# Up projection: ten column-tile pairs in seven block products, with their weight sums on GpSimd

## The chip, the core and the metric

The kernel runs on one core of one Trainium2 chip. Such a core has TensorE (PE: matmuls, with its weight loads listed apart as PEld), VectorE (DVE), ScalarE (ACT), GpSimd (POOL) and SyncE (SP, which here only issues DMAs). Each takes its own instructions in a fixed order and waits for the others through semaphores. The metric is the device time of one execution in microseconds, lower is better.

## The reference

One decoder layer on 512 tokens of 1024 channels, in float32. The part that the change touches is the channel mixer at the end:

```python
u2 = _rmsnorm(h, norm2_g[l])
z = _causal_dwconv(u2 @ w_ffn_up[l], ffn_dw_w[l], ffn_dw_b[l])
h = h + (jax.nn.silu(z[..., :FFN_DIM]) * z[..., FFN_DIM:]) @ w_ffn_down[l]
return _rmsnorm(h, final_g)
```

`w_ffn_up` is 1024 x 5632 (twice FFN_DIM = 2816), the convolution has width 3 along the tokens, `w_ffn_down` is 2816 x 1024. Before it come a norm, one input projection, a convolution branch with width 31, four heads of chunked gated linear attention, a gated merge of both branches and an output projection; of these the change touches only the end of the last attention head.

## The kernel before

**Precision.** A matmul is made of three matmuls in the fp32r format (`mm3`, L305): each operand is split into a rounded part `hi` and a rest `lo`, and lo x hi, hi x lo and hi x hi are added up in a PSUM bank. A weight tile of 128 x 1024 is loaded (`load`, L167, one 512 KB DMA into a `raw` tile, 4 buffers), then split by ScalarE (`whi`, L266) and VectorE (`wlo`, L267) in `split_weight`. The list `order` (L147 to L161) holds all weight tiles in the order of use; `weight` (L276) hands out the next one and splits two further ahead.

**Up projection.** It works on channels as rows and tokens as columns. `col_tile` (L313) makes one 128-channel column tile of the result: 8 blocks of the contraction, 3 matmuls each, all 512 tokens as the moving operand, so 24 matmuls of 128x512. Column tile i of the silu half and tile FT + i (FT = 22) of the gate half belong together: `glu` (L1106) runs the width-3 convolution (`ffn_conv`, L1098: one ScalarE instruction reading PSUM, two VectorE instructions), the silu and the product. The 22 pairs are taken in twos, (p, q): `first_of_pair` and `second_of_pair` (L1120, L1128) also build the sums of token halves that the down projection needs. There are three groups of such twos (`GROUPS`, L34: 4, 3 and 4 of them). After each group follows its part of the down projection.

**Down and output projection.** These already use the seven products of Strassen and Winograd in place of eight block products: `seven` (L979) with the steps a11, a12, s1, n2, s4, n3, a22. Their weight sums are made by DMAs that add while they write (issued by GpSimd, L208 and L225) and by VectorE (L218).

**Start of the up projection.** The first two (0, 2) is special (L1211 to L1220). Its four weight tiles are split beforehand, three of its four column tiles are made in token halves (128x256 matmuls) because the last tokens of `u2` arrive late (`to_channels`, L382, at the first halves of tiles 1 and 2), and the fourth is made whole:

```python
for j, lo in [(j, lo) for lo in (0, H) for j in range(3)]:
    ...
    col_tile(ws[j], acts2, accs[j], lo, lo + H, at)
col_tile(ws[3], acts2, accs[3])
```

**Order.** The code is written in one program order; a scheduler decides at compile time how the instructions of each engine follow each other, and the hardware then keeps that order. Where no `manual_schedule` or `issue_after` binds it, an instruction of a later line may be put ahead of an earlier one that is not ready in the scheduler's own reckoning.

**The last head.** `gated` (L875) transposes the head's output in two halves, the first into one of 5 `mm` PSUM banks, the second into one of 3 `ax` banks. At its last call (L916) four `mm` banks hold gate tiles (L906 to L915), so the next column tile (`w_gla`, L926) gets the bank of that first half.

**The end.** `Finish` (L1145) norms rows of the result: square sums on ScalarE, the gain product on VectorE, the root on GpSimd, then the scaling in two parts and a store. The last row block's last half is done in two pieces (L1027 to L1033). `gain3`, the final gain, is loaded at L1096, before the up projection.

Of the kernel before, what the change touches and what calls it, by code (L numbers as in the profile page):

```python
# [66 lines left out]
def trunk_layer(ctx: ExitStack, tc: tile.TileContext, a: dict, out: bass.AP):  # L67
# [55 lines left out]
    pp = cp.tile([P, PP_N], F32, name="pp")  # L123
    gate_up = cp.tile([P, HEADS * DK], F32R, name="gate_up")
    ones = cp.tile([P, P], F32, name="ones")
# [3 lines left out]
    keep = cp.tile([P, P], U8, name="keep")  # L129
    att = cp.tile([P, NT, P], F32, name="att")  # L130

# [27 lines left out]
    for gi, pairs in enumerate(GROUPS):  # L159
        order += [("w_up", j) for pair in pairs for i in pair for j in (i, FT + i)]  # L160
        order += [("w_down", (pairs, step, d)) for step, d in STEPS]  # L161
    ready, raws = [], []
    kept = {}
    used = [0]
    pace = [None]

    def load():  # L167
        if len(raws) < len(order):
            name, j = order[len(raws)]
            if name in SEVEN:  # L170
                raws.append(load_block(name, *j))
                return
            raw = raw_tile()
            nc.sync.dma_start(raw, a[name][j])
            raws.append(raw)

    def raw_tile():
        return wp.tile([P, D], F32, tag="raw", name=nm("raw"), bufs=4)
# [42 lines left out]
    def sum_on(name, pairs, step, d):  # L221

        if step in ("a11", "n2"):
            nxt = block(name, pairs, d, *((0, 1) if step == "a11" else (1, 0)))
            nc.gpsimd.dma_start(kept[pairs, d], nxt, accum_op=ALU.add)  # L225

    def split_weight(halves=False, between=None):

        if len(ready) < len(order):
            while len(raws) <= len(ready):  # L230
                load()
            raw = raws[len(ready)]
            name, spec = order[len(ready)]
            if name in SEVEN:
                raw = operand(raw, *spec)
# [5 lines left out]
                sum_on(name, *spec)  # L241
                ready.append((hi, lo))
                load()
                return
            hi = wp.tile([P, D], F32R, tag="whi", name=nm("whi"), bufs=4)
            if order[len(ready)][0] == "w_low":
                nc.scalar.copy(hi, raw)
                if order[len(ready)][1] == 0:
                    part_lo = lambda t: t.rearrange("p (k c) -> p k c", c=P)[:, :, :RANK]
                    nc.vector.tensor_tensor(part_lo(hi), part_lo(raw), part_lo(hi.bitcast(F32)), ALU.subtract)  # L250
                ready.append((hi, None))
                load()
                return
            lo = wp.tile([P, D], F32R, tag="wlo", name=nm("wlo"), bufs=4)
            if halves:
                ready.append((hi, lo))

                def high(c):
                    nc.scalar.copy(hi[:, c], raw[:, c])

                def low(c):
                    nc.vector.tensor_tensor(lo[:, c], raw[:, c], hi[:, c].bitcast(F32), ALU.subtract)

                cols = [slice(j * T, (j + 1) * T) for j in range(2)]
                return [[lambda c=c, part=part: part(c) for c in cols] for part in (high, low)]
            nc.scalar.copy(hi, raw)  # L266
            pace[0] = nc.vector.tensor_tensor(lo, raw, hi.bitcast(F32), ALU.subtract)  # L267
            ready.append((hi, lo))
            load()

# [41 lines left out]

    def col_tile(w, acts, acc=None, lo=0, hi=T, at={}):  # L313

        if acc is None:
            acc = mm_bank()
        for k in range(KT):
# [456 lines left out]
    class Head:  # L774
# [99 lines left out]

        def gated(self):  # L875
            for s in range(2):
                po = ax_bank() if s else mm_bank()
                for p in range(NT):
# [20 lines left out]
    for h in range(HEADS + 1):  # L899
# [15 lines left out]
        gate_r(2 * h + 1) if new else gate_b(3)  # L915
    heads[-1].gated()  # L916
    gla_scope.close()
# [61 lines left out]
    def seven(name, pairs, acts, complete, at=lambda step, i: None, fine=False):  # L979
# [31 lines left out]
        while steps:  # L1011
# [6 lines left out]
            for i in range(2):  # L1018
# [76 lines left out]
    ffn_scope, fp = scoped("ffn", 1)  # L1095
    gain3 = load_gain("final_g")  # L1096

# [22 lines left out]
    def first_of_pair(i, accs):  # L1120

        w = fp.tile([P, 3 * H], F32, tag="w", name=nm("w"), bufs=2)
        glu(i, accs, w[:, :T])
# [4 lines left out]
    def second_of_pair(i, accs, w, acts):  # L1128

        f = fp.tile([P, T], F32, tag="f", name=nm("f"), bufs=2)  # L1130
        glu(i, accs, f)
        v = fp.tile([P, 3 * H], F32, tag="v", name=nm("v"), bufs=2)
        s1, n2, s4 = (v[:, c * H : (c + 1) * H] for c in range(3))
# [6 lines left out]
        acts["s1"], acts["n2"], acts["s4"] = y(0), y(1), y(2)  # L1140
        return acts

    SPLIT = 5 * P

    class Finish:  # L1145
# [8 lines left out]
        def part(self, n, c):  # L1154
# [3 lines left out]
            y = self.y[:, n * T + c.start : n * T + c.stop] if self.y else tmp() if self.parts else hn  # L1158
            self.last = nc.vector.tensor_tensor(y, hn, gain3[:, n * T + c.start : n * T + c.stop], ALU.mult)
            self.parts.append((n, y))  # L1160
# [28 lines left out]
    def last_complete(t, n, c):  # L1189
# [3 lines left out]
        if ends[t].width == D and t > 1:  # L1193
            ends[t].scale()
            if t == 3:
                with tc.issue_after(ends[t].last.ins):
                    ends[2].store()
                ends[t].store()

    def last_at(step, i):  # L1200

        if (step, i) == ("a22", 0):
            for t in range(2):
                ends[t].scale()
            for t in range(2):
                ends[t].store()

    for gi, pairs in enumerate(GROUPS):
        acts = []
        early = {}  # L1210
        if gi == 0:  # L1211
# [10 lines left out]
        def both(i):  # L1222
            return early.get(i) or [col_tile(weight("w_up", i), acts2), col_tile(weight("w_up", FT + i), acts2)]

        for p, q in pairs:
            w, found = first_of_pair(p, both(p))
            acts.append(second_of_pair(q, both(q), w, found))
        if gi < len(GROUPS) - 1:
            seven("w_down", pairs, acts, lambda t, n, c: None)
        else:  # L1230
            seven("w_down", pairs, acts, last_complete, last_at, True)
    ffn_scope.close()
# [89 lines left out]
```

## Time and profile before

| | us |
|---|---|
| three timed runs: median (lowest, highest) | 837.88 (837.52, 839.6) |
| the profiled execution, its own device time | 837.71 |
| its span, first to last instruction | 835.9 |
| ScalarE, GpSimd busy in the span | 391.8, 42.9 |
| first two of the up projection, PE from its first matmul to the end of its fourth tile | 481.42 to 505.9 |
| first group's part of the down projection on PE | 571.4 to 609.5 |

The span is 1.8 us shorter than the device time of the same execution; what lies around it is not listed by instruction. In the trace a matmul's duration is from its start to its modelled end, and neighbours overlap: what a matmul costs in a stream is the distance between two starts. The same holds for VectorE and ScalarE, where a new instruction starts 0.06 to 0.1 us before the end that is listed for the one ahead of it.

### The profile page before, as it was taken

Reading aid. Unit: us, or ns where it says so; the run is one execution under the profiler, and the core shown is the slowest. Engines: PE = TensorE matmul, PEld = TensorE weight load, DVE = VectorE, ACT = ScalarE, POOL = GpSimd, SP = SyncE. Lnnn points to the kernel's source line nnn. Section 1 sums busy time; section 2 is a strip of 40 time slices with the busy share of each in tenths; the row PEclk is TensorE's granted clock in tenths of the full one; section 3 lists DMA queues with packets and bytes.
Section 4 is the critical chain, followed back from the end, with each engine's and each line's share of the span. In section 5 each row is a group of like instructions: output and inputs, shape, how many; then the busy total and the mean of one; then the engine's idle time right before and its main releaser. Section 6 shows DMA issues by size and latency. Waiting matters only on the chain.

```text
span 835.9 us, 9981 instructions
## 1 busy us (share of the span) xinstructions
PE 826.8 (99%) x3821; PEld 690.5 (83%) x3821; DVE 651.5 (78%) x927; ACT 391.8 (47%) x544; POOL 42.9 (5%) x65
## 2 busy tenths in 40 slices
PE   9999999999999999999999999999999999999996
PEld 7888888888888888888888898888888888888885
DVE  6689879999998788744688868778757687677795
ACT  6632247437523422449434554444434444444454
POOL 1000000000000100000001000001000010000111
PEclk9999999999999999999999999999999999999999
DMA  8233322222222322222347643234742348322462
GB/s 313 101 102 101 101 99 86 98 79 76 101 76 76 126 100 86 92 101 76 106 96 220 205 155 112 91 98 103 216 150 88 67 89 285 102 84 93 101 125 102
DMA packets 28305, 97.79 MB, mean 117 GB/s; under 512 B 3208, under 2 KB 3344, under 8 KB 28256
## 3 DMA queue, kind: packets, MB, share of 16 engines
q1 hardware_dynamic: 24800, 85.35, 29.6%
q0 software_dynamic: 3456, 11.80, 8.2%
q8 instruction: 30, 0.49, 0.2%
q14 instruction: 19, 0.16, 0.1%
HBM read 95.03 MB, written 2.10 MB: 116 GB/s over the span
## 4 chain that ended last, share of the span: by engine, by line
PE 96%; DVE 1%; ACT 0%; DMA 0%; issue 0%; POOL 0%; POOLq 0%; SPq 0%; ACTq 0%
PE mm L309 29%; PE mm L310 29%; PE mm L311 29%; PE mm L521 3%; PE ax L862 1%; PE ax L310 1%; PE ax L311 1%; PE ax L309 1%; PE ax L864 1%; PE ax L844 1%; PE ax L435 0%; PE ax L831 0%; PE ax L830 0%; DMA x<-in_x_dram 0%; DVE hres L1023 0%
## 5 line engine op out<-in xcount | busy, mean ns | idle before, releaser
L309 PE MATMUL mm<-uh,wlo 128*128 128x512 f32 (+1 forms) x760 | 293.0, 385 | 0.0
L311 PE MATMUL mm<-uh,whi 128*128 128x512 f32 (+1 forms) x760 | 290.8, 383 | 0.0
L310 PE MATMUL mm<-ul,whi 128*128 128x512 f32 (+1 forms) x760 | 290.6, 382 | 0.0
L266 ACT CAST whi<-raw 128x1024 fp32r<-128x1024 f32 x114 | 118.7, 1046 | 125.5 <-PE mm L311 93.6
L267 DVE TENSOR_TENSOR wlo<-raw,whi 128x1024 fp32r<-128x1024 f32 x114 | 138.4, 1218 | 36.7 <-ACT whi L266 36.4
L311 PEld LDWEIGHTS mm<-uh,whi 128*128 128x128 f32 x760 | 142.8, 188 | 27.9
L310 PEld LDWEIGHTS mm<-ul,whi 128*128 128x128 f32 x760 | 142.9, 188 | 27.6
L309 PEld LDWEIGHTS mm<-uh,wlo 128*128 128x128 f32 x760 | 142.9, 188 | 27.6
L615 DVE SCALAR_TENSOR_TENSOR c<-h,pp,c 128x511 f32<-128x511 f32 (+14 forms) x240 | 162.4, 728 | 0.7
L1103 DVE SCALAR_TENSOR_TENSOR tmp<-mm,pp,tmp 128x511 f32<-128x511 f32 x88 | 65.9, 748 | 68.8 <-ACT tmp L1101 67.5
L1101 ACT ACTIVATE tmp<-mm,pp 128x512 f32<-128x512 f32 x44 | 34.3, 780 | 61.8 <-PE mm L311 61.8
L239 ACT CAST whi<-kept 128x1024 fp32r<-128x1024 f32 (+1 forms) x32 | 31.7, 995 | 24.0 <-DVE kept L218 10.6
L240 DVE TENSOR_TENSOR wlo<-kept,whi 128x1024 fp32r<-128x1024 f32 (+1 forms) x32 | 36.6, 1152 | 3.0 <-ACT whi L239 2.8
L1023 DVE TENSOR_TENSOR hres<-hres,mm 128x512 f32<-128x512 f32 (+1 forms) x49 | 32.7, 671 | 5.0 <-PE mm L311 3.3
L239 ACT CAST whi<-raw 128x1024 fp32r<-128x1024 f32 (+1 forms) x24 | 23.7, 995 | 18.0 <-PE mm L311 17.8
L240 DVE TENSOR_TENSOR wlo<-raw,whi 128x1024 fp32r<-128x1024 f32 (+1 forms) x24 | 27.3, 1152 | 2.4 <-ACT whi L239 2.3
L310 PE MATMUL mm<-wlo,sh 128*128 128x512 f32 x66 | 25.8, 391 | 0.0
L311 PE MATMUL mm<-whi,sh 128*128 128x512 f32 x66 | 25.7, 389 | 0.0
L309 PE MATMUL mm<-whi,sl 128*128 128x512 f32 x66 | 25.5, 389 | 0.0
L309 PE MATMUL mm<-h,wlo 128*128 128x512 f32 x64 | 25.0, 391 | 0.4 <-DVE tmp L882 0.4
L310 PE MATMUL mm<-h,whi 128*128 128x512 f32 x64 | 24.9, 389 | 0.0
L311 PE MATMUL mm<-h,whi 128*128 128x512 f32 x64 | 24.9, 389 | 0.0
(258 smaller groups left out, 1127.9 us busy)
## 6 DMA issues: line engine op xcount, KB each, us to landing
raw<-in_w_up_dram SPq DMA_DIRECT2D x44, 512.0 KB, 3.3
raw<-in_w_glu_dram SPq DMA_DIRECT2D x16, 512.0 KB, 3.9
raw<-in_w_down_dram SPq DMA_DIRECT2D x15, 512.0 KB, 3.3
kept<-in_w_down_dram POOLq DMA_DIRECT2D x10, 512.0 KB, 5.4
raw<-in_w_v_dram SPq DMA_DIRECT2D x8, 512.0 KB, 3.8
raw<-in_w_qk_dram SPq DMA_DIRECT2D x8, 512.0 KB, 3.3
raw<-in_w_r_dram SPq DMA_DIRECT2D x8, 512.0 KB, 3.3
raw<-in_w_gb_dram SPq DMA_DIRECT2D x8, 512.0 KB, 3.1
```

The lines of the kernel that those rows point to most:

```text
L239: nc.scalar.copy(hi, raw)
L240: nc.vector.tensor_tensor(lo, raw, hi.bitcast(F32), ALU.subtract)
L266: nc.scalar.copy(hi, raw)
L267: pace[0] = nc.vector.tensor_tensor(lo, raw, hi.bitcast(F32), ALU.subtract)
L309: nc.tensor.matmul(acc, ll, rh, start=first, stop=False, **kw)
L310: nc.tensor.matmul(acc, lh, rl, start=False, stop=False, **kw)
L311: nc.tensor.matmul(acc, lh, rh, start=False, stop=last, **kw)
L521: nc.tensor.matmul(acc, act, ready[k // 2][wi][:, j], start=first, stop=last)
L615: nc.vector.scalar_tensor_tensor(y[:, s:], c[:, : T - s], w, y[:, s:], ALU.mult, ALU.add)
L1023: nc.vector.tensor_tensor(hres[t, n][:, c], hres[t, n][:, c], acc[:, c], op)
L1101: nc.scalar.activation(z, acc, AF.Identity, bias=pp[:, PP_FB + m : PP_FB + m + 1], scale=w[2])
L1103: nc.vector.scalar_tensor_tensor(z[:, s:], acc[:, : T - s], w[j], z[:, s:], ALU.mult, ALU.add)
```

## The change

For ten of the eleven twos (p, q), all but the first, the column tiles q and FT + q are no longer made as two column tiles. Their 1024 x 256 weights are taken as 2 x 2 blocks (halves of the contraction; tile q and tile FT + q) and the activations as 2 x 2 blocks (halves of the contraction; token halves), and seven block products of 12 matmuls 128x256 take the place of eight. Tiles p and FT + p stay plain. The products are interleaved in program order with half tiles of FT + p and of the next p. GpSimd makes the weight sums (`up_sums`: four additions of 128x512 per pair). The sums of the activations are made once (`sum_acts`), after `first_of_pair` of the first two. Results are put together in two SBUF tiles, from which the convolution then reads. Further: loads run 2 ahead and not 4 from the second two of a group on (`refill`), several buffers go from 2 to 1, `gate_up` and `att` move to a pool that is freed earlier, `gated` uses an `ax` bank for both halves in its last call, `gain3` is loaded before the last down projection, and at the end the order of the two last pieces is fixed by hand and the store of row block 2 is written between them.

```diff
+    def up_order(pairs):
+        out = []
+        for n, (p, q) in enumerate(pairs):
+            if n == 0:
+                out.append(("w_up", p))
+            out += [("w_up7", (q, "x1")), ("w_up", FT + p), ("w_up7", (q, "x3")), ("w_up7", (q, "x2"))]
+            if n + 1 < len(pairs):
+                out.append(("w_up", pairs[n + 1][0]))
+            out.append(("w_up7", (q, "x4")))
+        return out
...
+    def refill():
+        while len(raws) < len(order):
+            few = len(raws) >= first7 and order[len(raws)][0] != "w_down"
+            if len(raws) >= len(ready) + (2 if few else 4):
+                return
+            load()
...
+    def up_sums(q, part):
+        add = lambda out, x, y: nc.gpsimd.tensor_tensor(out, x, y, ALU.add)
+        left, right = slice(0, T), slice(T, D)
+        if part == "x1":
+            one, two = pair_raws[q]
+            three = raw_tile()
+            pair_raws[q].append(three)
+            add(three[:, left], one[:, left], two[:, left])
+            add(three[:, right], three[:, left], two[:, right])
+            add(two[:, left], two[:, left], two[:, right])
+        if part == "x3":
+            one, _, three = pair_raws[q]
+            add(three[:, left], three[:, right], one[:, right])
...
-                po = ax_bank() if s else mm_bank()
+                po = ax_bank() if s or last else mm_bank()
...
-                    add(n, acc, slice(0, H))
-                    add(n, rest, slice(H, T))
+                    with tc.manual_schedule(engines={ET.DVE, ET.Activation}):
+                        add(n, acc, slice(0, H))
+                        add(n, rest, slice(H, T))
...
+    def sum_acts():
...
+        src = {step: room(step) for step in ("n3", "s1", "n2")}
+        chain(nc.gpsimd, src["n3"], a11[0], (sub, a21[0]), (add, a11[1]), (sub, a21[1]))
+        chain(nc.vector, src["s1"], a21[0], (sub, a22[0]), (add, a21[1]), (sub, a22[1]))
+        chain(nc.vector, src["n2"], src["s1"], (sub, a11[0]), (sub, a11[1]))
+        seven_acts["s1"] = split_sum(src["s1"], hi["s1"], lo["s1"])
+        src["s4"] = room("s4")
+        chain(nc.vector, src["s4"], src["n2"], (add, a12[0]), (add, a12[1]))
+        for step in ("n2", "n3", "s4"):
+            seven_acts[step] = split_sum(src[step], hi[step], lo[step])
...
+    def up_pair(q):
+        x, y, z = mm_bank(), ax_bank(), ax_bank()
+        c1, c2 = tmp(), tmp()
...
+        w = weight("w_up7", (q, "x1"))
+        up_step(x, "a11", w, 0, True)
+        put(c1[:, t1], x)
+        up_step(z, "a12", w, 1, True)
+        combine(c1[:, t1], c1[:, t1], z[:, :H], ALU.add)
+        yield
+        w = weight("w_up7", (q, "x3"))
+        up_step(x, "n2", w, 1, False)
+        put(c2[:, t1], x)
+        up_step(y, "s1", w, 0, True)
+        put(c2[:, t2], y)
+        yield
+        w = weight("w_up7", (q, "x2"))
+        up_step(x, "n3", w, 0, False)
+        combine(c2[:, t2], c2[:, t2], x[:, :H], ALU.subtract)
+        up_step(y, "s4", w, 1, False)
+        combine(c2[:, t1], y[:, :H], c2[:, t1], ALU.subtract)
+        yield
+        up_step(x, "a22", weight("w_up7", (q, "x4")), 0, False)
+        put(c1[:, t2], x)
+        yield [c1, c2]
...
-            early = {pairs[0][0]: accs[:2], pairs[0][1]: accs[2:]}
...
-        for p, q in pairs:
-            w, found = first_of_pair(p, both(p))
-            acts.append(second_of_pair(q, both(q), w, found))
+            p, q = pairs[0]
+            w, found = first_of_pair(p, accs[:2])
+            sum_acts()
+            acts.append(second_of_pair(q, accs[2:], w, found))
+
+        half = [range(KT // 2), range(KT // 2, KT)]
+        rest = pairs[gi == 0 :]
+        acc = col_tile(weight("w_up", rest[0][0]), acts2)
+        for n, (p, q) in enumerate(rest):
+            parts = up_pair(q)
+            next(parts)
+            wt = weight("w_up", FT + p)
+            gate = col_tile(wt, acts2, ks=half[0])
+            next(parts)
+            col_tile(wt, acts2, gate, ks=half[1])
+            w, found = first_of_pair(p, [acc, gate])
+            next(parts)
+            if n + 1 < len(rest):
+                wt = weight("w_up", rest[n + 1][0])
+                acc = col_tile(wt, acts2, ks=half[0])
+            done = next(parts)
+            if n + 1 < len(rest):
+                col_tile(wt, acts2, acc, ks=half[1])
+            acts.append(second_of_pair(q, done, w, found))
...
-            if t == 3:
-                with tc.issue_after(ends[t].last.ins):
-                    ends[2].store()
-                ends[t].store()
+        if t == 3 and n == 0:
+            ends[2 if c.start == 0 else 3].store()
```

In `split_sum` ScalarE rounds a sum to `hi` (128x1024) and VectorE subtracts to get `lo`; `up_step` issues the 12 matmuls of one block product; `put` is a ScalarE copy and `combine` a VectorE addition or subtraction, each 128x256.

More of the change, by code (lines that the diff above doesn't have):

```diff
@@ L129, in trunk_layer @@
     keep = cp.tile([P, P], U8, name="keep")
-    att = cp.tile([P, NT, P], F32, name="att")
+    att = gp.tile([P, NT, P], F32, name="att")
     def load_consts():
@@ L172, in load @@
                 return
+            if name == "w_up7":
+                q, part = j
+                if part == "x1":
+                    pair_raws[q] = [raw_tile() for _ in range(2)]
+                    for raw, m in zip(pair_raws[q], (q, FT + q)):
+                        nc.sync.dma_start(raw, a["w_up"][m])
+                raws.append(None)
+                return
             raw = raw_tile()
@@ L240, in split_weight @@
                 nc.vector.tensor_tensor(lo, raw, hi.bitcast(F32), ALU.subtract)
-                sum_on(name, *spec)
+                sum_on(name, *spec) if name in SEVEN else up_sums(*spec)
                 ready.append((hi, lo))
-                load()
+                refill()
                 return
@@ L251, in split_weight @@
                 ready.append((hi, None))
-                load()
+                refill()
                 return
@@ L268, in split_weight @@
             ready.append((hi, lo))
-            load()
+            refill()
     def prefetch(n):
@@ L311, in mm3, with col_tile @@
         nc.tensor.matmul(acc, lh, rh, start=False, stop=last, **kw)
[L313 removed]
+    def col_tile(w, acts, acc=None, lo=0, hi=T, at={}, ks=range(KT)):
         if acc is None:
             acc = mm_bank()
[L317 removed]
+        for k in ks:
             s = slice(k * P, (k + 1) * P)
@@ new lines, in up_step, with put, combine @@
+    def up_step(acc, step, w, half, opens):
+        ah, al = seven_acts[step]
+        for k in range(4):
+            s = slice(half * T + k * P, half * T + (k + 1) * P)
+            mm3(acc[:, :H], (w[0][:, s], w[1][:, s]), (ah[k], al[k]), opens and k == 0, k == 3, not opens)
+    def up_pair(q):
+        x, y, z = mm_bank(), ax_bank(), ax_bank()
+        c1, c2 = tmp(), tmp()
+        t1, t2 = slice(0, H), slice(H, T)
+        def put(c, acc):
+            nc.scalar.copy(c, acc[:, :H])
+        def combine(c, l, r, op):
+            nc.vector.tensor_tensor(c, l, r, op)
+        w = weight("w_up7", (q, "x1"))
[19 more added lines that the diff above has]
+        yield [c1, c2]
```

64 lines of the change are left out of this document (50 added, 14 removed).

## The prediction

> **What bounds the kernel now.** I read the page's first part, then who PE waited for, then windows and timelines by engine around the stages that change.
>
> ```profile
> span 835.9 us, 9981 instructions
> ...
> PE 826.8 (99%) x3821; PEld 690.5 (83%) x3821; DVE 651.5 (78%) x927; ACT 391.8 (47%) x544; POOL 42.9 (5%) x65
> ```
> ```profile
> PE mm L427 <- DVE ones L400: 1.1, 1, 1.1
> PE mm L309 <- DVE tmp L882: 0.4, 1, 0.4
> PE mm L521 <- ACT h L448: 0.3, 1, 0.3
> ```
>
> The second view lists all of PE's waits with their totals: 1.8 us, none of it in the up projection. So a matmul saved is time saved and a new PE wait is time lost. Windows (columns: stretch and length, then busy us and count of PE, PEld, DVE, ACT, POOL, granted clock, DMA share, GB/s) of the first two's fourth column tile and of one later two (96 matmuls):
>
> ```profile
> 500.45:505.90 5.45, 5.45 (x26) 4.51 (x25) 5.41 (x8) 3.27 (x5) 0.00 (x0) 1.00 0.39 140
> 549.64:571.40 21.76, 21.76 (x97) 18.02 (x96) 15.47 (x21) 10.11 (x14) 1.75 (x2) 1.00 0.43 96
> ```
>
> A 128x512 matmul costs 21.76/96 = 0.2267 us. DVE is busy for 71% of a later two, but for 99% of the fourth tile of the first two: there it already has nothing to spare.
>
> **Part 1, the matmuls.** The 128x256 form runs before too, in the first two:
>
> ```profile
> 482.01 0.28 PE L311 MATMUL mm<-uh,whi 128*128 128x256 f32 x1
> ...
> 487.05 0.28 PE L311 MATMUL mm<-uh,whi 128*128 128x256 f32 x1
> ```
>
> These starts are 42 matmuls apart: 5.04/42 = 0.120 us each, a little over half of 0.2267. Per two, 48 x 0.2267 = 10.88 us become 84 x 0.120 = 10.08 us. Ten times 0.80: **-8.0 us**. The weight loads (one per matmul) keep that pace in the same stretch. The saving is gone at 10.88/84 = 0.1295 us per matmul.
>
> **Part 2, the first two.** `sum_acts` stands in program order between `first_of_pair` and everything that comes next. The order compiled into the changed kernel, read from its program, has on DVE, after the last `to_channels` subtraction: three sums for s1; then, mixed, four sums for n2 and s4, eight convolution steps, w and its difference, and the `lo` parts of s1, n2, n3, s4 and y; and only as the 24th instruction the `lo` part of the next column tile's weights. In the kernel before, that kind of split is the third. PE's first matmul after the fourth tile needs it, and nothing may pass it on PE. DVE's timeline before:
>
> ```profile
> 491.08 1.29 DVE L393 TENSOR_TENSOR ul<-ax,uh 128x512 fp32r<-128x512 f32 x2 [1.37 <-ACT uh L392]
> 495.70 1.53 DVE L1103 SCALAR_TENSOR_TENSOR tmp<-mm,pp,tmp 128x511 f32<-128x511 f32 x2 [3.33 <-ACT tmp L1101]
> 497.15 1.21 DVE L267 TENSOR_TENSOR wlo<-raw,whi 128x1024 fp32r<-128x1024 f32 x1
> ```
>
> The last subtraction ends at 492.37. Prices (start to start): a 1024 subtraction 1.13 (578 to 600 us are full of them), about 1.23 where it waits for its predecessor; 512 wide 0.60; a convolution step 0.725; w's difference 0.35. The 24: 7 sums x 1.23 = 8.6; 4 x 1.13 = 4.5; 4 of 512 (two halves of n3, y, w) = 2.4; 8 x 0.725 = 5.8; 0.35: 21.7 us. DVE cannot be done before 492.4 + 21.7 = 514.1, and PE wants the split at 505.9: **at least 8.2 us of new PE wait**. It is charged once; all later work shifts by it.
>
> It grows through GpSimd. ACT's compiled order puts the two rounding copies of n3, whose sum GpSimd makes in three additions of 1024, ahead of the convolution's first ACT step, and DVE's convolution waits for that. GpSimd can start at 491.65, when ACT has written the last `uh`. With P per addition the convolution starts on DVE at 491.65 + 3P + 1.95 (two copies 0.55 each, one ACT step, the handover), and 17.9 us of the 21.7 are behind it: wait = 5.6 + 3P. No wide two-input GpSimd operation is in the trace; the nearest rows, and DVE's own such sum:
>
> ```profile
> L144 POOL MEMSET att<- 128x512 f32 x1 | 0.5, 524 | 0.0
> ...
> L134 POOL MEMSET shares<- 128x128 f32 x1 | 0.2, 204 | 0.0
> ```
> ```profile
> L218 DVE TENSOR_TENSOR kept<-kept,raw 128x1024 f32<-128x1024 f32 x7 | 8.5, 1219 | 0.0
> ```
>
> One pass of GpSimd is (524 - 204)/384 = 0.83 ns per column: P is 0.95 with one pass (then the 8.2 of DVE decides, 8.5 us), 2.6 with three. I take two passes, one per input: P = 1.8, 11.0 us. The trace also shows that a GpSimd operation is held up by a DVE one:
>
> ```profile
> 480.72 0.55 POOL L359 TENSOR_TENSOR rstd<-var,mhalf 128x1 f32<-128x1 f32 x1 [7.58 <-DVE var L1060]
> ...
> 484.70 1.37 POOL L359 TENSOR_TENSOR rstd<-var,mhalf 128x1 f32<-128x1 f32 x1 [3.42 <-DVE var L1060]
> ```
>
> The same operation takes 0.55 us beside an idle DVE and 1.37 beside the `wlo` subtraction that runs from 484.44 to 485.66, ending 0.4 behind it. If the three additions alternate with DVE's three s1 sums, two DVE sums of 1.2 come on top: 13.4 us. I take the middle, **+12.2 us**; bounds 8.2 and 5.6 + 3 x 2.6 + 2.4 = 15.8.
>
> [...]
>
> **The clock behind the wait.** Windows behind PE's last matmul (828.8), and the opening's weight loads:
>
> ```profile
> 831.00:832.00 1.00, 0.00 (x0) 0.00 (x0) 0.47 (x1) 0.54 (x1) 0.00 (x0) 1.00 1.00 414
> 832.00:833.00 1.00, 0.00 (x0) 0.00 (x0) 0.00 (x0) 0.00 (x0) 0.00 (x0) 0.57 0.89 365
> 833.00:834.00 1.00, 0.00 (x0) 0.00 (x0) 0.00 (x0) 0.00 (x0) 0.00 (x0) 0.50 0.66 270
> ```
> ```profile
> 1.12 3.06 PEld L427 LDWEIGHTS mm<-ones 128*128 128x128 f32 x14 [1.12 <-DVE ones L400]
> ...
> 6.34 0.75 PEld L427 LDWEIGHTS mm<-ones 128*128 128x128 f32 x6
> ```
>
> The granted clock falls to half about 3.4 us after PE goes idle. At the opening 14 warming matmuls take 0.22 us each, later six take 0.125: some 3.4 us at half rate. A wait over 8 us ends the same way: half of 3.4 is lost, **+1.7 us** (bounds 0 and 3.4, two such stretches).
>
> **Part 3, the later twos.** Added per two: 1.5 weight splits (1.13 each on DVE, 0.95 on ACT) and three combines (0.35); DVE comes to 15.47 + 1.7 + 1.05 = 18.2 us of a 20.96 us period (four halves of plain tiles 10.88, products 10.08). Laid out against PE with the row prices, every split lands 5.5 us or more before its matmul, the DMAs (3.3 us) and GpSimd's sums before that: nothing on the path. GpSimd's four additions of 512 (0.95 each by two passes) can push DVE by up to 3.8, to 22.0 us, 1.0 over the period; the 5.5 us of slack takes that in groups of three or four: **+0.5**, bounds 0 and 3.
>
> At each entry into the down projection the chain of the last q is longer: a `put`, two ACT steps, four convolution steps and the silu come behind the last product, where before the silu half was convolved 5.4 us earlier. Before, DVE ended that q's last split (`sl`) 10.2 us after the down projection's first matmul (581.4 against 571.2); laid out, it now ends 15.0 after, and s1's second half wants it at 14.4. About 0.5 three times: **+1.5**, bounds 0 and 5.
>
> **Part 4, the ends.** The `w_gla` tile no longer waits for the bank: **-0.4** (the wait on L882 above); oa[6] and oa[7] are still ready 1.2 and 0.6 us before their matmuls. At the end the store of row block 2 leaves about 1.2 us earlier (830.2 before), but its DVE scaling now stands ahead of the last piece's addition and costs that 0.15: **-0.2**, bounds -0.5 and +0.2. The gain's later load (4.3 us) is on SP behind the last w_down loads and lands while a11 and a12 run: nothing; without that cover 4 us. `refill` cuts loads to 2 ahead, 3.3 us against at least 4 us between splits: nothing.
>
> **Sum**, against the profiled execution's 837.71 (0.17 below the median of the runs, so no correction): -8.0 + 12.2 + 1.7 + 0.5 + 1.5 - 0.4 - 0.2 = +7.3, so 845.0 us.
>
> **Rivals.**
> - *A short wait.* GpSimd's additions take about 1 us and do not hold DVE: wait 8.5, clock 1.7, entries 0.5: 837.7 - 8.6 + 10.7 = 839.8. For it: the 0.524 memset; against: an addition reads two inputs.
> - *DVE becomes the bound.* Three passes on GpSimd, and DVE stands still for each: 15.8 in the first two, 3.4 for the clock, 3 in the twos, 3 at the entries: 837.7 - 8.6 + 25.2 = 854. Decided by whether DVE passes 21 us per two. [...]
> - *Faster: the split is not behind the sums.* If that `lo` part ran as early as before, PE would meet only the x3 split and the n2 sums: wanted at 505.9 + 5.44 + 2.88 + 2.72 = 516.9, ready near 520: 3 us, too short to drop the clock. 837.7 - 8.6 + 3 + 1 = 833. It needs VectorE to leave its compiled order or to do those 24 in 14 us; the 1.2 us rows speak against it.
> - *The products save nothing:* 0.1295 us or more per matmul beside DVE and GpSimd traffic: 853. The steady 0.120 speaks against it.
>
> **Numbers.** The forecast (841 to 850) 0.56, short wait 0.16, DVE bound 0.13, split ahead 0.12, no saving 0.03. Faster or slower means by over 0.3% (2.5 us, about what a measurement of this kernel can tell from none). Faster 0.12; same 0.16; slower 0.72. The range 835 to 853 leaves out the faster case and the tail of the DVE bound. The likeliest case's own is 841 to 850.
>
> **What would show it.** Right: one PE wait of 11 to 14 us on DVE's `wlo` near 506, then matmuls at twice their distance for some 3 us; 256-wide starts 0.120 apart in the later twos; small waits at the three entries; GpSimd additions of about 1.8 us (1024) and 0.95 (512); no wait at L926. Wrong: no such wait (the reading of DVE's order failed), or waits spread over all ten twos (DVE is the bound).

## The result and the profile after

| | before | after |
|---|---|---|
| median of the runs, us (lowest, highest; 4 runs each) | 837.7 (837.49, 839.6) | 858.88 (858.16, 859.41) |
| profiled execution, us | 837.71 | 858.53 |
| its span, us | 835.9 | 856.5 |

The changed kernel takes 1.0252 times as long (95% interval 1.0239 to 1.0265). The direction was predicted; the size, 21.2 us, was three times the predicted 7.3 and outside the range.

The first part of the page after:

```profile
span 856.5 us, 10963 instructions
...
PE 825.7 (96%) x4181; PEld 703.4 (82%) x4181; DVE 706.8 (83%) x989; ACT 424.5 (50%) x609; POOL 119.2 (14%) x108
```

PE is busy 1.1 us less than before in a span that is 20.6 us longer: it waits. Its waits (engine and line, who was waited for, total, times, longest, all in us):

```profile
PE mm L361 <- DVE wlo L319: 13.4, 1, 13.4
PE mm L361 <- DVE yl L1169: 6.7, 3, 2.3
PE mm L361 <- DVE hres L1075: 1.1, 1, 1.1
```

The first is the predicted wait behind the first two. The second, three waits at the three entries into the down projection, is not in the prediction in this size. The third is one short wait some 24 us behind the second entry.

A ledger says where all of the time is. It takes the distances between the starts of neighbouring PE matmuls and subtracts the prices of the kernel before (0.2267 us for 512 columns, 0.120 for 256); what is left over is time that PE lost. It is cut into stretches:

| term | predicted, us | measured, us |
|---|---|---|
| products instead of column tiles | -8.0 | -8.0 |
| wait behind the first two (505.06 to 518.81) | +12.2 | +13.5 |
| slow clock behind it (518.8 to 525) | +1.7 | +2.9 |
| the later twos, three stretches (0.19, 0.19, 0.27) | +0.5 | +0.65 |
| the three entries (2.74, 6.07, 3.56) | +1.5 | +12.4 |
| head and end | -0.6 | -0.45 |
| the same kind of loss in the kernel before | | -0.2 |
| sum | +7.3 | +20.8 |

The last PE matmul starts 20.63 us later than before, so the ledger closes. Of 13.9 us that the prediction missed, 10.9 are at the entries.

**The products.** The first and the last of the twelve 128x256 matmuls of one step in PE's timeline, eleven distances apart (the rows between them are the other ten):

```profile
576.28 0.28 PE L361 MATMUL ax<-xs,wlo 128*128 128x256 f32 x1
...
577.61 0.28 PE L363 MATMUL ax<-xs,whi 128*128 128x256 f32 x1
```

1.33/11 = 0.121 us per matmul: the saving is there.

**The first wait.** GpSimd's and DVE's timelines at the sums of the activations (start, duration, engine, line, operation, count; where a count is 2 the duration is that of both):

```profile
490.50 2.40 POOL L1215 TENSOR_TENSOR raw<-uh 128x1024 f32<-128x1024 f32 x1 [5.09 <-ACT uh L444]
492.98 6.61 POOL L1215 TENSOR_TENSOR raw<-raw,ul 128x1024 f32<-128x1024 f32 x2
```
```profile
491.66 2.32 DVE L1215 TENSOR_TENSOR kept<-uh,uh 128x1024 f32<-128x1024 f32 x1
494.02 6.65 DVE L1215 TENSOR_TENSOR kept<-kept,ul 128x1024 f32<-128x1024 f32 x2
...
517.55 1.21 DVE L319 TENSOR_TENSOR wlo<-raw,whi 128x1024 fp32r<-128x1024 f32 x1
```

A DVE sum that takes 1.22 us alone takes 2.32 and then 3.3 beside GpSimd, and GpSimd's go from 2.40 to 3.3: the two take turns. The split that PE waits for ends at 518.76. This is the mechanism that was predicted, with the turns; how the price of 13.4 came out is said below.

**The entries.** The chain of work from 575 to 592 us, first entry (start, duration, what):

```profile
582.11 5.38 DMA kept<-in_w_down_dram
587.49 0.02 issue
587.51 0.03 ACT whi L291
587.54 0.92 issue
588.47 0.62 ACT yh L1168
589.09 0.02 issue
589.11 0.70 DVE yl L1169
589.81 0.04 issue
589.86 0.50 PE mm L361
```

The adding DMA that GpSimd issues after a11's split (L257) needs 5.38 us; the pages list this DMA at a median of 5.4 us before and 5.6 after. ScalarE's rounding copy of its result, for step s1, which PE wants only 36 matmuls, 8 us, after the first of the down projection, stands in ScalarE's compiled order ahead of `yh`, which PE wants at once. So `yh` waits for a DMA that it has nothing to do with, `yl` waits for `yh`, and PE for `yl`, from 587.5 to 589.86. The other two entries read alike (DMA landing at 691.5 and 810.2); at the second one VectorE's half of the same split (`wlo`, 692.62 to 693.85) also goes ahead of `yl`. VectorE's a11 split and ScalarE's s1 copy, first before and then after:

```profile
558.15 1.22 DVE L240 TENSOR_TENSOR wlo<-kept,whi 128x1024 fp32r<-128x1024 f32 x1
572.08 1.04 ACT L239 CAST whi<-kept 128x1024 fp32r<-128x1024 f32 x1
```
```profile
580.54 1.22 DVE L292 TENSOR_TENSOR wlo<-kept,whi 128x1024 fp32r<-128x1024 f32 x1
587.51 1.04 ACT L291 CAST whi<-kept 128x1024 fp32r<-128x1024 f32 x1 [2.16 <-DMA kept<-in_w_down_dram]
```

In the kernel before, a11's first split ends 11.8 us ahead of the down projection's first matmul (559.37 against 571.20), with whole plain tiles of 5.44 us in between; its DMA landed at 565.19, long before the copy. Now the split ends 3.0 us ahead of that matmul (581.76 against 584.78) and 5.8 us ahead of 587.54, where PE wants the last two's `yl`.

Of the 6.07 us at the second entry 2.4 are the wait, 1.7 a stretch at half clock, and 1.3 the wait on `hres` at 718: there the adding DMA behind n2 (709.15 to 716.95) holds a copy, its split and a VectorE addition that PE needs.

### The profile page after: what moved, and what is told of

Same layout as the page of the kernel before. It is cut to its first block, busy times and chain, and to the rows that moved or that the text cites. A ratio compares the mean times of both kernels' runs of the same rounds, so it can differ in the third digit from the quotient of the medians.

```text
span 856.5 us, 10963 instructions
## 1 busy us (share of the span) xinstructions
PE 825.7 (96%) x4181; PEld 703.4 (82%) x4181; DVE 706.8 (83%) x989; ACT 424.5 (50%) x609; POOL 119.2 (14%) x108
## 4 chain that ended last, share of the span: by engine, by line
PE 71%; DVE 12%; issue 7%; ACT 3%; DMA 3%; POOL 3%; POOLq 0%; SPq 0%; ACTq 0%
PE mm L361 20%; PE mm L362 20%; PE mm L363 20%; DVE tmp L1155 3%; DMA kept<-in_w_down_dram 3%; PE mm L573 3%; DVE wlo L292 3%; POOL raw L266 2%; POOL raw L1215 1%; DVE hres L1075 1%; ACT whi L291 1%; DVE wlo L319 1%; PE ax L361 1%; PE ax L363 1%; PE ax L362 1%
## 5 line engine op out<-in xcount | busy, mean ns | idle before, releaser
L361 PE MATMUL mm<-uh,wlo 128*128 128x512 f32 (+1 forms) x680 | 255.1, 375 | 13.4 <-DVE wlo L319 13.4
L362 PE MATMUL mm<-ul,whi 128*128 128x512 f32 (+1 forms) x680 | 252.5, 371 | 0.0
L363 PE MATMUL mm<-uh,whi 128*128 128x512 f32 (+1 forms) x680 | 252.1, 371 | 0.0
L318 ACT CAST whi<-raw 128x1024 fp32r<-128x1024 f32 x94 | 98.2, 1048 | 133.8 <-PE mm L363 90.8
L361 PEld LDWEIGHTS mm<-uh,wlo 128*128 128x128 f32 x680 | 129.0, 190 | 35.1 <-DVE wlo L319 13.8
L363 PEld LDWEIGHTS mm<-uh,whi 128*128 128x128 f32 x680 | 128.8, 189 | 22.3
L319 DVE TENSOR_TENSOR wlo<-raw,whi 128x1024 fp32r<-128x1024 f32 x94 | 114.9, 1225 | 36.7 <-ACT whi L318 36.5
L292 DVE TENSOR_TENSOR wlo<-raw,whi 128x1024 fp32r<-128x1024 f32 x64 | 75.2, 1182 | 14.9 <-ACT whi L291 14.8
L291 ACT CAST whi<-raw 128x1024 fp32r<-128x1024 f32 x64 | 60.9, 961 | 24.3 <-PE mm L363 15.6
L266 POOL TENSOR_TENSOR raw<-raw,raw 128x512 f32<-128x512 f32 x30 | 48.2, 1606 | 156.2 <-DVE wlo L292 112.0
L1155 DVE SCALAR_TENSOR_TENSOR tmp<-mm,pp,tmp 128x511 f32<-128x511 f32 (+1 forms) x48 | 35.5, 745 | 19.3 <-ACT tmp L1153 19.1
L1155 DVE SCALAR_TENSOR_TENSOR tmp<-tmp,pp,tmp 128x511 f32<-128x511 f32 (+1 forms) x40 | 34.6, 924 | 0.0
```

The costliest lines, as they stand in the source:

```text
L266: add = lambda out, x, y: nc.gpsimd.tensor_tensor(out, x, y, ALU.add)
L361: nc.tensor.matmul(acc, ll, rh, start=first, stop=False, **kw)
L362: nc.tensor.matmul(acc, lh, rl, start=False, stop=False, **kw)
L363: nc.tensor.matmul(acc, lh, rh, start=False, stop=last, **kw)
L1155: nc.vector.scalar_tensor_tensor(z[:, s:], acc[:, : T - s], w[j], z[:, s:], ALU.mult, ALU.add)
```

## The experiments

Twelve kernels ran, each beside the kernel before. All ratios are to the kernel before.

| kernel | median, us (runs) | ratio, 95% interval | PE lost, us: from 500 to 550 / from 550 on |
|---|---|---|---|
| changed kernel | 858.88 (4) | 1.0252, 1.0239 to 1.0265 | 16.5 / 12.9 |
| 1 no adding DMA behind a11 | 850.73 (4) | 1.0153, 1.0135 to 1.017 | 16.5 / 5.4 |
| 2 one copy behind yh | 854.64 (4) | 1.0207, 1.0184 to 1.023 | 16.4 / 9.2 |
| 3 two copies, behind yh and ah | 852.35 (4) | 1.0174, 1.016 to 1.0188 | 16.7 / 6.8 |
| 4 one GpSimd sum of three | 852.74 (1) | | 11.3 / 12.2 |
| 5 n3's sum on VectorE | 854.19 (1) | | 12.7 / 12.6 |
| 6 splits ahead of the sums | 853.4 (4) | 1.0174, 1.015 to 1.0197 | 9.9 / 15.1 |
| 7 second two plain | 848.51 (4) | 1.0127, 1.0112 to 1.0142 | 5.5 / 12.2 |
| 8 second plain, sums later, two copies | 840.81 (4) | 1.0035, 1.0021 to 1.0048 | 2.4 / 8.3 |
| 9 before, head and end alone | 836.89 (11) | 0.9992, 0.9983 to 1.0001 | 0 / 0.2 |
| 10 seven such twos, two copies | 838.45 (11) | 1.001, 1.0 to 1.0021 | 0 / 5.6 |
| 11 five such twos | 833.0 (5) | 0.9952, 0.9938 to 0.9966 | 0 / 0.6 |
| 12 six such twos | 833.65 (5) | 0.9954, 0.994 to 0.9967 | 1.2 / 0.6 |

The last column is from the ledger of each kernel's profile. Its second figure holds the three entries and some 0.5 us that is spread over all the rest; a ledger's difference and that of the medians differ by up to 1 us, since the opening of the kernel varies from run to run.

### The entries: experiments 1 to 3

**1.** In the changed kernel the adding DMA behind a11 is left out:

```diff
-        if step in ("a11", "n2"):
+        if step == "n2" or (step == "a11" and name == "w_o"):
```

> The changed kernel without the adding DMA behind a11 in the down projection, so the weights of s1, n2 and a22 lack one summand in all three groups. Theory (at each entry ScalarE's copy of s1's weights waits 2.2 us for that DMA, and yh, yl and PE queue up behind it): PE's three waits on DVE yl, 6.7 us in all, fall under 1 us, the half-clock stretch after the second of them goes too, 7 to 10 us less than the changed kernel: 849 to 852. Rival (the longer chain of the last q, a put, four convolution steps and the silu, sets the entries): waits of 5 us or more stay at the entries, now on other tiles: 855 to 859.

Measured: 850.73, 8.2 us less by the medians, 7.6 by the ledger. PE's waits at the entries:

```profile
PE mm L361 <- DVE sl L1169: 1.5, 1, 1.5
...
PE mm L361 <- DVE yl L1169: 0.8, 3, 0.3
```

The waits on `yl` fall from 6.7 to 0.8, and the half-clock stretch behind the second of them is gone, with the 1.1 us on `hres` as well. What the rival names is there too, but smaller: `sl`, the end of the last q's chain, is waited for once, 1.5 us. So some 60% of the entries' 12.4 us hang on that DMA.

**2.** The DMA stays; ScalarE's copy of s1's first weights is tied behind `yh`:

```diff
-                nc.scalar.copy(hi, raw)
+                if name == "w_down" and spec[1:] == ("s1", 0):
+                    with tc.issue_after(rounded[0].ins):
+                        nc.scalar.copy(hi, raw)
+                else:
+                    nc.scalar.copy(hi, raw)
```

> The changed kernel with one order fixed: ScalarE's copy of s1's first weights stands behind the yh copy of the last two; the adding DMA stays. Theory (only the place of that copy in ScalarE's queue matters): yl is ready before PE wants it, the 6.7 us of waits fall under 1, s1's own weights are still in time (copy near 589, wanted some 10 us after the entry): 849 to 852, the same as without the DMA within 1 us. Rival (DMA late for s1 itself, or the chain of the last q): a wait of 2 us or more per entry moves to s1's weights or to hres: 855 to 859.

Measured: 854.64, 4.2 less, between the two ranges. The chain at the third entry:

```profile
802.77 8.77 DMA kept<-in_w_down_dram
...
811.62 1.05 ACT whi L296
812.67 0.53 ACT ah L1173
813.20 0.02 issue
813.22 0.69 DVE al L1176
```

`yh` is now ahead, and the next copy of the same kind, for s1's second half, stands ahead of `ah` and waits for a DMA of 8.77 us. DVE's splits queue up behind `al`, and PE loses 2.3 us there. The wait moved one step down the same queue. The rival was nearer in time, by 0.4 us, but the wait is on a12's second weights (split at 815.10, behind `al`), not on s1's or on `hres`, as it had it.

**3.** Both copies are tied, to `yh` and to `ah`:

```diff
+                if name == "w_down" and spec[1] == "s1":
+                    with tc.issue_after(rounded["ya"[spec[2]]].ins):
+                        nc.scalar.copy(hi, raw)
```

> The changed kernel with ScalarE's two copies of s1's weights bound behind yh and ah of the group's last two; all DMAs stay. Without the adding DMA the changed kernel was 8.2 us shorter; with the first copy alone behind yh 4.2, and there a second copy waited for a DMA of 8.8 us ahead of ah. Theory (only the place of the two copies in ScalarE's queue matters, not the DMA's time): 7 to 9 us less than the changed kernel, 850 to 852, no wait over 1.6 us at the three entries. Rival (s1's weights themselves come too late behind the DMA): 2 us or more per entry stay, 853 to 856.

Measured: 852.35, 6.5 less, just outside the theory's range; the longest wait at an entry is 0.9 us. All DMAs are in place and as slow as before, so the place of the copies in ScalarE's queue, not the transfer as such, makes most of the loss (6.2 us by the ledger); 1.4 more go when the transfer goes too.

### The first two: experiments 4 to 7

**4.** GpSimd does one addition of three for n3's sum:

```diff
-        chain(nc.gpsimd, src["n3"], a11[0], (sub, a21[0]), (add, a11[1]), (sub, a21[1]))
+        chain(nc.gpsimd, src["n3"], a11[0], (sub, a21[0]))
```

> The changed kernel with one GpSimd operation of 128x1024 in place of three for n3's sum (the two lo terms of that sum are left out). Theory (GpSimd's chain holds ScalarE's n3 copies, these the convolution, and it takes turns with VectorE): the wait at 506 falls from 13.4 to 8.2 to 9.5 us, the bound by VectorE's own 24 instructions plus one turn. Rival (VectorE's work alone sets the wait, GpSimd is beside it): 12 to 13.4 us stay. The half-clock stretch stays at 2.5 to 3 us in both.

```profile
PE mm L361 <- DVE wlo L319: 8.2, 1, 8.2
```

```profile
491.87 2.32 DVE L1215 TENSOR_TENSOR kept<-uh,uh 128x1024 f32<-128x1024 f32 x1
```

The wait falls to 8.2. That is the number that the prediction gave for VectorE alone, but not its case: the one addition left on GpSimd still costs VectorE 1.1 us (the row above, 2.32 in place of 1.22). VectorE alone would come to some 7.1 us, an estimate from these two figures.

**5.** `chain(nc.vector, src["n3"], ...)`: VectorE makes that sum as well.

> The changed kernel with n3's sum moved from GpSimd to VectorE (three more sums of 1.2 us there, none on GpSimd between 490 and 505). Theory (GpSimd's part in the wait is its own slow, mutually blocking additions): VectorE's queue ahead of the split grows from 21.7 to 24.6 us, so the wait is 10.5 to 12 us, less than the 13.4 with GpSimd's help. Rival (the 13.4 is VectorE's own work and what ScalarE adds, and GpSimd was help): 14 to 17 us.

```profile
PE mm L361 <- DVE wlo L319: 9.6, 1, 9.6
```

The direction is the theory's, the wait 0.9 us below its range: PE waits 3.8 us less with all of the sums on VectorE than with GpSimd's help. Some 0.7 us of that need not be GpSimd's doing: in this kernel's compiled order one of the eight convolution steps (0.66 us) stands behind the split and no longer ahead of it.

**6.** The next splits are written ahead of the sums:

```diff
+            prefetch(2)
             sum_acts()
```

> The changed kernel with the splits of the next column tile and of the first seven-product weights written ahead of the sums of the activations. Theory (the 13.4 us wait is DVE's queue order: 24 instructions ahead of one split): PE goes on at 506 and meets the sums only at the x3 step, wanted at 516.9 and ready near 519 to 521: a wait of 2 to 4 us there, with no half clock or one: 845 to 850. Rival (VectorE beside GpSimd has too much work whatever its order): the wait comes back at x3, x2 or in the next two, 8 us or more in all: 853 to 859.

Measured: 853.4 (850.78 to 853.86), in the rival's range. PE goes on at once but waits 1.7 and 5.8 us later. The second of these, in ScalarE's timeline:

```profile
527.67 1.14 ACT L1223 CAST btmps<-raw 128x512 fp32r<-128x512 f32 x2 [11.09 <-POOL raw L1215]
528.72 0.83 ACT L1168 CAST sh<-v 128x768 fp32r<-128x768 f32 x1
529.45 0.36 ACT L1261 COPY tmp<-mm 128x256 f32<-128x256 f32 x1
```

ScalarE stands for 11 us at the copy of n3's sum, which GpSimd now starts only at 515.83, and behind it in the queue is the copy (L1261) that empties the bank PE needs. It is the pattern of the entries again, with GpSimd in the DMA's place. The theory overlooked it.

**7.** The second two stays plain (nine in products) and the sums are written into it:

```diff
-        rest = pairs[gi == 0 :]
+        rest = pairs[2 * (gi == 0) :]
...
+            p, q = pairs[1]
+            w, found = first_of_pair(p, [col_tile(weight("w_up", j), acts2) for j in (p, FT + p)])
+            sum_acts()
```

> The changed kernel with the second two of the first group left plain (nine seven-product twos in place of ten, 0.8 us less saved) and the sums of the activations written into that two. Theory (the first two's wait is work in the wrong place, not work that cannot be hidden): 13.4 of wait and 2.9 of slow clock go, up to 3 us come back where the sums meet the first convolutions: 843 to 847. Rival (25 us of sums do not fit beside two plain twos): waits of 6 us or more on DVE between 506 and 535: 849 to 856.

Measured: 848.51, 10.4 less, 1.5 over the theory's range and just under the rival's; one wait of 3.5 us at 528 with 1.6 of slow clock behind it is left of 16.5.

### Both together, and the parts alone: experiments 8 to 12

**8.** Experiment 7 with the sums written behind the first column tile of the third two, and the two copies of experiment 3.

> The changed kernel with three edits: the second two plain (nine seven-product twos), the sums of the activations written behind the first column tile of the third two, and ScalarE's two copies of s1's weights behind yh and ah. Theory (the loss is two places of queue order, and the products do save 0.8 us each): 7.2 saved by the products, 0.45 by the head, 1 to 4 us of short waits at the entries and 0 to 3 where the sums meet the x3 products: 832 to 838, at or below the kernel before. Rival (VectorE beside GpSimd cannot hold the sums even under a plain two): 5 us or more of waits between 506 and 545: 839 to 846.

Measured: 840.81, in the rival's range, though the waits between 506 and 545 come to 2.3 us and not 5. GpSimd's n3 sum stands behind the weight sums of the third two and again holds ScalarE, for 5.1 us ahead of its copy at 534.95; another 1.5 us is lost at 570, and the entries cost what they did in 3.

**9.** In the kernel before, only the head and the end are reordered, with the same lines as in the change.

> The kernel before with only the two reorderings: the ax bank in the last head, and the order of the last two pieces with the store between them. Theory (the bank's wait was 0.4 us on the path, the end gives nothing): 0.3 to 0.5 us faster, 837.2 to 837.5. Rival (predicted with the end at -0.2 too): 0.6 to 0.8 faster, or no change if the head's gain is eaten by the next tile.

Measured: 836.89 against 837.45; the interval reaches from 0.17% faster to 0.01% slower. It holds the theory's 0.45 us and nothing at all: not told apart.

**10 and 11.** The first group is plain, with the sums behind its second two. In 10 the other two groups are as changed (`PLAIN_END = (0, 0, 0)`), with the two tied copies of experiment 3; in 11 their last twos are plain too, and nothing is tied. The lines of 11:

```diff
+PRE = 4
+PLAIN_END = (0, 1, 1)
+def sevens(gi):
+    return GROUPS[gi][PRE * (gi == 0) : len(GROUPS[gi]) - PLAIN_END[gi]]
...
-        order += up_order(pairs[gi == 0 :])
+        order += up_order(sevens(gi))
+        order += [("w_up", j) for two in pairs[len(pairs) - PLAIN_END[gi] :] for i in two for j in (i, FT + i)]
```

> The changed kernel with seven seven-product twos: the first group plain, its second two carrying the sums of the activations, the other two groups as changed, and ScalarE's two copies of s1's weights bound behind yh and ah. Theory (the rest at an entry is 2.7 in the group of three and 2.1 in the last, as with ten twos and that order): -5.6 for the products, -0.45 for the head, +4.8 at the entries: 836 to 838, less good than five twos with covered entries. Rival (the entries' rest came from the congestion behind the first two): 833 to 835.

> The changed kernel with five seven-product twos in place of ten: the first group plain, its second two carrying the sums of the activations, and the last two of the other groups plain; no order bound by hand. Theory (each entry was covered by whole plain tiles, and the sums by plain twos): no wait over 0.5 us on yl or sl at any entry, though the adding DMAs stay; -4.0 for the products, -0.45 for the head, 0 to 2 us of small waits: 833 to 836, faster than the kernel before by 0.2 to 0.5%. Rival (seven products cost elsewhere too, or the entries wait for the DMA however the weights are laid): 837.5 to 842.

Measured: 838.45 (runs from 836.57 to 841.77) for seven twos, 0.45 over the theory's range and no faster than the kernel before, though the 2.9 and 2.2 us lost at the two entries are near the theory's; 833.0 for five, faster than the kernel before by 0.48% (0.34 to 0.62). The page and PE's waits of experiment 11:

```profile
span 831.3 us, 10486 instructions
...
PE 822.9 (99%) x4001; PEld 696.3 (84%) x4001; DVE 683.8 (82%) x964; ACT 409.1 (49%) x579; POOL 82.3 (10%) x88
```
```profile
PE mm L488 <- DVE ones L461: 1.1, 1, 1.1
PE ax L496 <- DMA x<-in_x_dram: 0.2, 1, 0.2
```

Those two are the whole list, both in the opening. The last PE matmul starts 4.49 us earlier than before (824.00 against 828.49). Of this 0.90 lie ahead of the up projection, whose first matmul starts at 480.52 and not at 481.42. The 3.59 that are left, and 0.4 that this kernel's ledger loses more than that of the kernel before, make 4.0: five times 0.80. So the products give all that they promise where the two costs are gone. At its entry into the second group's down projection (PE 672.2), DVE's and ScalarE's timelines show the split of a11 and the copy that waits for the DMA:

```profile
660.44 1.22 DVE L301 TENSOR_TENSOR wlo<-kept,whi 128x1024 fp32r<-128x1024 f32 x1
```
```profile
673.08 1.04 ACT L300 CAST whi<-kept 128x1024 fp32r<-128x1024 f32 x1
```

There are 11 us between the end of the one and the start of the other, and no wait stands behind the copy's row: the plain last two gives the DMA its cover back, with ScalarE's order as the compiler made it.

**12.** Experiment 11 with the third two of the first group in products (`PRE = 2`, `PLAIN_END = (1, 1, 1)`) and n3's sum on VectorE.

> As the version with five seven-product twos, with the third two of the first group in seven products too (six in all, the last two of every group plain) and n3's sum on VectorE. Theory (with n3's sum off GpSimd the sums fit under one plain two, and a plain last two covers the first entry): 0.8 less than with five if the sums meet no product, up to 2 more if they do: 832 to 834.5. Rival (as with the sums behind one plain two before, 3.8 us of waits near 537 and 570 stay): 835 to 837.

Measured: 833.65, in the theory's range. The sixth saving is eaten by a wait of 0.8 us near 548; five and six cannot be told apart by their intervals.

## Why the prediction was wrong in size

**Part 1, the products (-8.0): right.** The distances of the changed kernel and the ledger of experiment 11 both give 0.80 us per two.

**Part 2, the first two's wait (+12.2): right, 13.4.** It came on the instruction, line and place that were named, and experiments 4 and 5 show that GpSimd's turns are in it. That the case with the turns, priced at 13.4, is met to 0.1 us is luck: GpSimd's three additions took 9.1 us (490.50 to 499.59) and not 7.8 (3 x 1.8 + 2.4), but they started at 490.50 and not at 491.65, so that the convolution began at 501.47 as priced (501.4). What follows was shorter by 0.6 us (17.3 from there to the end of the split, 17.9 priced), and PE was done with the fourth tile 0.45 us earlier, which nearly cancels too. VectorE's own bound of 8.2 was too high, by some 1.1 us (experiment 4): the first of its sums starts at 491.66 and not at 492.37, and a convolution step takes 0.66 us and not 0.725. The mis-sized input is GpSimd's addition: 1.8 us for 1024 columns and 0.95 for 512 were taken, 2.40 and 1.29 are its durations where nothing holds it up. The case with the turns had a better sum than the middle: here VectorE is held up beside GpSimd, 2.32 against 1.22 us.

**The clock (+1.7): right in kind, 2.9 in size.** The 3.4 us at half rate was an estimate: behind the wait PE ran at half clock from 518.81 to 524.75, 5.9 us, and in the kernel before the opening's matmuls stand 0.21 us apart or more until 6.10, 5.0 us behind the first of them, and about 0.11 from there. One more stretch at half clock came at the second entry, 1.7 us lost, which no term had. The prediction took a wait of 3 us as too short to drop the clock; here one of 2.2 us did.

**Part 3, the later twos (+0.5): right, 0.65.** VectorE did not become the bound. That GpSimd's additions push it by up to 3.8 us, to 22.0, was an estimate that no run shows: in the two periods of 20.96 us from 539.69 on it was busy for 18.6 and 19.7.

**Part 3, the entries (+1.5, bounds 0 and 5): the step that failed; 12.4.** It laid out the last q's convolution chain alone. It did not ask what each copy in ScalarE's queue waits for, and its DMAs were the plain loads of 3.3 us: the copy of s1's weights waits for an adding DMA of 5.4 us that plain tiles had covered and that now holds `yh` until 588.47, 2.3 us after VectorE has its operand ready (L1176 ends at 586.18). Experiment 1 puts 7.6 us on that DMA, and experiments 2 and 3 show that it works through the place of two copies in the queue. Some 4.5 us remain at the entries in experiment 1. Of these 1.5 are a wait on `sl`, the end of the chain that was priced at 1.5 for all three entries, and 0.8 waits on `yl`; the rest lies in short losses whose cause stays open.

**Part 4 (-0.6): about right, -0.45.** No wait is left at the `w_gla` tile, and the fourth tile ends 0.45 us earlier (505.45 against 505.9). That difference alone would not show the gain: in the profiles of the thirteen kernels with the new head, the up projection starts anywhere from 480.41 to 481.99, before at 481.42. The end gives nothing, 7.4 us from the start of the last PE matmul to the end of the span in both.

**The rivals.** *A short wait* and *split ahead* fall with the 13.4 us. *The products save nothing* falls with the 0.121 us. *DVE becomes the bound* came nearest in time, 854, and is wrong as a cause: no wait spreads over the twos. No rival named a DMA behind which a queue stands, though the page before has its price: a split that ends 5.8 us ahead of the place where PE wants `yl` leaves a transfer of 5.4 us, and the 2.3 us of the copy, `yh` and `yl` behind it, no room.

## What to carry to other kernels

When a change shortens the work that one look-ahead step spans, price again every wait that this span covered, the slow asynchronous ones first (adding DMAs, GpSimd chains): for each instruction of an in-order queue list what it waits for and what stands behind it, also where it is itself not urgent. Keep plain, long tiles where such latencies need cover, and put the short ones where nothing hangs on them: five savings without a wait beat ten with. Moving work to an idle engine is no gain where the two engines hold each other up (a wait of 13.4 us with GpSimd's help, 9.6 without); time both together.

## What the runs showed of the hardware

**The granted clock changed on a grid.** Windows of the changed kernel, 3.41 us each, on the grid on which its granted clock changed, around the first entry (two rows) and the second (three rows); PE's busy time is the first figure behind the length, the granted clock the third from the end:

```profile
586.19:589.61 3.42, 1.50 (x7) 0.92 (x5) 1.63 (x2) 2.10 (x3) 0.02 (x1) 1.00 0.95 170
589.61:593.02 3.41, 3.17 (x14) 2.63 (x15) 3.41 (x6) 2.05 (x4) 0.00 (x0) 1.00 0.53 174
...
692.00:695.41 3.41, 1.17 (x6) 0.77 (x5) 2.79 (x4) 3.05 (x5) 0.00 (x0) 1.00 0.53 162
695.41:698.82 3.41, 3.41 (x10) 2.63 (x9) 3.20 (x6) 1.34 (x3) 0.84 (x1) 0.50 0.27 34
698.82:702.23 3.41, 3.41 (x17) 2.81 (x16) 3.41 (x8) 1.23 (x2) 0.00 (x0) 1.00 0.65 126
```

Two waits of nearly the same length (2.16 and 2.24 us): the first is cut by the grid and cost nothing more, the second lies inside one window and was followed by a whole window at half clock, ten matmuls in place of 15, 1.7 us lost. From 500 us on the granted clock of this profile changed at 507.68, 524.75, 695.41, 698.82 and 852.42 us, that is 5, 50, 1 and 45 times 3.413 us apart. Of its windows at full clock up to the last matmul, two held 2.23 and 2.24 us of PE idle (from 504.27 and from 692.00) and were followed by half clock; the one with the next most, 1.90 us (from 586.19), was not. At half clock, the window with 0.90 us of PE idle (517.93 to 521.34) was followed by half clock, the two without any (from 521.34 and from 695.41) by full clock. In experiments 4 and 5 PE lost 2.0 us at the first entry, and its matmuls went on at their usual distance; it lost 2.1 to 2.3 at the other two, and behind each of these seven or eight matmuls stood 0.42 to 0.43 us apart. So some 2.2 us of idle in one window was enough here, and a wait of 2.2 us cost 2.2 at one entry and 3.9 at another.

**The adding DMA was slow and uneven:** 512 KB took 5.38 us from issue to landing at the first entry and 8.77 in experiment 2; the plain loads of that size on the page after have medians of 3.1 to 3.9.

**VectorE starved GpSimd as well as alternating with it.** In the stretch from 491 to 501 us above, where each of VectorE's sums reads the one before it, the two took turns and both were slowed. From 518.7 to 523.2 us VectorE ran an unbroken row of seven instructions at their usual lengths (1.22 us for a split), and GpSimd's two additions of 512 columns, 1.29 us each alone, took 6.50 together. What decides between the two was not tried.
